# A hybrid encoder block with a mixture of experts: program order kept through the k and q projections, small copies and shifts moved between engines, and the end of the expert loop written in another order

## The chip, the cores and the metric

The kernel runs on one core of a Trainium2 chip. Times are device microseconds (us) of one execution. TensorE multiplies, VectorE, ScalarE and GpSimd do the elementwise work, and SyncE issues nearly all DMA transfers; in the profile they are PE, DVE, ACT, POOL and SP. The program of each engine is a list that the engine works off in order.

## The reference, cut to what matters

```
h = rmsnorm(x, mix_norm)                       # x: 512 rows x 1024
q, k, v, f_logit, gate_in, rec_in = split(h @ w_in)
log_f = log_sigmoid(f_logit + b_forget)
att = forgetting_attention(q, k, v, log_f)     # 8 heads of 64, causal softmax, bias by cumulated log_f
rec = causal_depthwise_conv(rec_in, conv_w, conv_b)
rec = rg_lru(rec, w_a, b_a, w_x, b_x, lam)     # gated linear recurrence over the rows
lru_out = rec * gelu(gate_in)
x = x + concat(att, lru_out) @ w_out
h2 = rmsnorm(x, ffn_norm)
# experts: 4 groups of 8; every row goes to the best group and to the best 2 experts in it
hg = silu(h2 @ w_gate[e]) * (h2 @ w_up[e])     # 1024 -> 256
y += (hg * combine[e]) @ w_down[e]             # 256 -> 1024
out = rmsnorm(x + y, final_norm)
```

All arrays are float32. The weights of the 32 experts are 100 MB, and every expert's weights are read once.

## The kernel before, in words

**Front.** The 512 rows stand as 4 tiles of 128. A product that wants full precision is made from three matmuls (`mm3`): both operands are split in a rounded high part (a copy on ScalarE, `split` by `act`) and a low part (a subtraction on VectorE or, for one tile at the start, on GpSimd), and high x high, high x low and low x high are added in PSUM. First come the rows' norm, their transposes (`hT`) and the v projection, whose weights `load_wv(half, kk)` brings in four pieces; then 16 projection chunks j of 128 columns (`chunk_gen(j)`): j = 0 to 3 feed the recurrent branch, 4 to 7 are k, 8 to 11 are q, 12 to 15 the gate. `chunk_gen(j)` loads and splits the weights of chunk j+1 (one `slot<-slot` of 128x1024 on ScalarE, one on VectorE), issues the 24 matmuls of chunk j (`ps_mm<-slot`) and then stores: `store_k` does on ScalarE, VectorE and ScalarE the three steps kS (high part), kS of the other half (low part) and kC (copy), twice; `store_q` one copy to qT. With j = 2 to 5 `gates` makes the gates of the recurrence, and from j = 8 on `next(rc)` issues a piece of the recurrence `recur()`: for each of 4 column blocks a tanh (a2th<-hold,ns), an exp (hold<-hold,s) and a square (a2th<-hold) on ScalarE and two products on VectorE, two blocks in a piece; then one square root over 128x2048 behind a load of its table; then four products and scans on VectorE.

**Attention.** There are 32 items (8 heads x 4 row tiles). For each pair of heads `stage_q` splits q: `qh` is copied by ScalarE, copied again by VectorE to the other half of the partitions (line 557, a cast), and GpSimd makes the low part `qC`. `logits` runs three matmuls, takes the row maximum on VectorE (nb), shifts it by two cumulated biases (a `TENSOR_SCALAR` of 128x1 on VectorE), and gives it to the exp on ScalarE as its bias. Then the row is normalised, transposed (ps_tr) and weighs v. Two strings of digits say how many matmul pieces of the output projection, the gate chunks and the router are put between the items.

**Experts.** The experts run as 8 "quads" of 4 experts; the last two (group 3, called light) have one set of places instead of two. A quad needs 12 MB of weights, through a ring of 18 buffers of 1 MB (slot, slot_m, slot_b): the gate and up weights (`load_gate_up`), then the down weights (`load_down`). A quad runs 8 steps k of gate and up matmuls (`gu_k`), multiplies the gated value (`hidden`, waits on ScalarE and VectorE), transposes it (`hidden_T`, ps_tr<-ident,hg), runs the down matmuls (`down`, ps<-slot,hgT), splits the result (y) and scatters it back with 0/1 matrices (`places` builds them, sT; ps_lg<-y,sT), each product added to xs by VectorE. The second half of a quad's scatter is kept back (`held`) and issued behind step k = 0 of the quad after. The last quad ends in the final norm: squares on ScalarE, a root and Newton step, and eight writes of the output (`write_out`).

**What sets the order.** Loads keep the program's order on SyncE's queue. With `pinned[0]` at 0 a scheduler sets the order of the engines' instructions; at 1 TensorE's instructions keep the program's order, at 2 those of VectorE and ScalarE that go through the helpers too. The loads of expert weights wait for ring buffers that the work before gives back.

Of the kernel before, what the change touches and what calls it, by code (L numbers as in the profile page):

```python
# [18 lines left out]
P = 128  # L19
# [34 lines left out]
def block_kernel(ctx, tc, x, mix_norm, w_in, b_forget, conv_w, conv_b, w_a, b_a, w_x, b_x, lru_lambda,  # L54
# [195 lines left out]
    raws = [load_wv(0, 0)]  # L250
    load_x(1)
    raws.append(load_wv(0, 1))
# [309 lines left out]
    def logits(qb, hd):
# [12 lines left out]
        ts(nb, nb, c1, ALU.subtract, c1, ALU.add)  # L575
# [423 lines left out]

    def places(g, q, hfs, s16):  # L1000

        n = NS * 3 if g else 12
        pt = pst("gz")
        pc = pst("tr")[:, 0:n] if len(hfs) > 1 else pt[:, 2 * P:2 * P + n]
        sq = [(2 * h + t, s16[h][:, t, q * 4:q * 4 + 4, :].rearrange("p e c -> p (e c)")) for h in hfs for t in range(2)]
        rows = [slice(e * CAP, (e + 1) * CAP) for e in range(4)]
        for i, (t, v) in enumerate(sq):
# [6 lines left out]
        sT = {}  # L1014
        for i, h in enumerate(hfs):
            sT[h] = ring_b[0].tile([P, 2, P], F32R, name=f"sT{h}", bufs=1)
            act(sT[h], pt[:, 2 * i * P:2 * (i + 1) * P].rearrange("p (t s) -> p t s", t=2), AF.Copy)
# [16 lines left out]
        return sT, cw  # L1034
# [136 lines left out]
    for i, (g, q) in enumerate(quads[:-1]):  # L1171
# [107 lines left out]
    scatter_to(pb, y0, sT[1])  # L1279
    for t in range(2):  # L1280
# [3 lines left out]
    down_mm(py1, hgT, dns[i], 1, [1])  # L1284
    y1 = split_y(py1)
    for t in range(2, 4):
        square_out(t, 0, xs[:, t, h0])
    pc, pd = ([psum("lg"), psum(tag)] for tag in ("mm", "tr"))
    scatter_to(pc, y1, sT[0])
    scatter_to(pd, y1, sT[1])  # L1290
    n0, n1 = (rsqrt_parts(hf) for hf in range(2))
    for t in range(2):
        scatter_add(pc[t], t, 1)
        square_out(t, 1, xs[:, t, h1])
    for t in range(2):
        scatter_add(pd[t], 2 + t, 1)
    i0 = next(n0)
    run(n0)
    for t in range(2, 4):
        square_out(t, 1, xs[:, t, h1])  # L1300
    write_out(0, 1, i0, xs[:, 0, h1])
    i1 = next(n1)
    run(n1)
    for t in range(NT):
        if t:
            write_out(t, 1, (i0, i1)[t // 2], xs[:, t, h1])
        write_out(t, 0, (i0, i1)[t // 2], None)
# [88 lines left out]
```

## Time and profile before

| | |
|---|---|
| median of 3 runs | 493.54 us (492.54 to 494.38) |
| profiled execution, its own time | 493.44 us |
| span of its trace | 491.6 us |
| mean granted TensorE clock | 0.983 of full speed |
| PE busy | 456.8 us, 93% of the span |
| DVE busy | 300.2 us, 61% |
| ACT busy | 200.7 us, 41% |
| POOL busy | 42.3 us, 9% |
| moved by the main DMA queue | 120.56 MB |

The shares are means over stages with different limits: the front runs to about 260 us, the experts from there to the end. The span leaves out 1.8 us of the profiled execution's time.

### The profile page before, as it was taken

The page shows a single profiled execution, that of the slowest core. Times are in us where ns is not written, and L with a number is a line of the kernel's source. Part 1 is how long each engine was busy: PE and PEld are TensorE (multiplying, and loading weights), DVE is VectorE, ACT ScalarE, POOL GpSimd, SP SyncE. Part 2 cuts the span into 40 slices and gives each one's busy share as a digit, 9 for nine tenths or more (in the row PEclk, how much of TensorE's full clock was granted, in tenths as well). Part 3 has the DMA queues.
Part 4 walks back from the last instruction along what each step waited for, and adds up shares of the span by engine and source line. Part 5 has one row for each costly group of instructions (what it writes and reads, how often), then busy time and mean ns, then how long its engine had stood idle before and what let it go on. Part 6 is the DMA issues. An engine that isn't in the chain of part 4 may idle for free.

```text
span 491.6 us, 9352 instructions
## 1 busy us (share of the span) xinstructions
PE 456.8 (93%) x3481; PEld 282.3 (57%) x3481; DVE 300.2 (61%) x768; ACT 200.7 (41%) x414; POOL 42.3 (9%) x84
## 2 busy tenths in 40 slices
PE   5999999899999999999999999999999999998880
PEld 3998777688876776668834345333354343633330
DVE  5768885653899477896675735346363363353553
ACT  6546669834685175655433123111131111211243
POOL 4500000011221012201000000000000000000040
PEclk9999999999999999999999999999999999999985
DMA  8767323042219230058879999999999999999934
GB/s 313 150 161 187 86 60 102 11 129 86 87 50 330 44 135 0 1 173 321 264 243 346 404 365 384 409 408 408 381 413 408 407 409 380 398 406 378 318 133 174
DMA packets 60883, 121.20 MB, mean 247 GB/s; under 512 B 11010, under 2 KB 29474, under 8 KB 60835
## 3 DMA queue, kind: packets, MB, share of 16 engines
q1 hardware_dynamic: 60832, 120.56, 68.9%
q8 instruction: 29, 0.48, 0.4%
q14 instruction: 20, 0.16, 0.1%
q10 hardware_dynamic: 2, 0.00, 0.0%
HBM read 118.45 MB, written 2.10 MB: 245 GB/s over the span
## 4 chain that ended last, share of the span: by engine, by line
PE 82%; DVE 10%; ACT 5%; issue 1%; DMA 1%; DVEq 0%; ACTq 0%
PE ps_mm L69 49%; PE ps_lg L69 16%; PE ps_tr L69 11%; PE ps_pv L69 3%; PE ps_tr L79 3%; ACT hold L94 1%; DVE h2l L88 1%; DVE hg L88 1%; DVE xs L82 1%; DVE nb L574 1%; DMA xs<-in_x_dram 1%; ACT kS L94 1%; DVE s L82 1%; ACT slot L94 1%; ACT hg L94 1%
## 5 line engine op out<-in xcount | busy, mean ns | idle before, releaser
L69 PE MATMUL ps_mm<-slot 128*128 128x512 f32 (+1 forms) x576 | 122.2, 371 | 3.8 <-ACT kC L94 2.3
L69 PEld LDWEIGHTS ps_mm<-slot 128*128 128x128 f32 x576 | 98.2, 196 | 23.4 <-ACT kC L94 2.7
L69 PE MATMUL ps_mm<-slot,xg 128*32 128x512 f32 x688 | 102.2, 594 | 0.0
L69 PEld LDWEIGHTS ps_mm<-slot,xg 128*32 128x32 f32 x688 | 25.7, 110 | 38.2 <-issue 36.3
L82 DVE TENSOR_TENSOR xs<-xs,ps_lg 128x512 f32<-128x512 f32 x61 | 38.1, 682 | 13.4 <-PE ps_lg L69 13.2
L82 DVE TENSOR_TENSOR slot<-slot 128x1024 fp32r<-128x1024 f32 (+1 forms) x27 | 32.7, 1221 | 12.1 <-ACT slot L94 11.9
L94 ACT ACTIVATE hg<-ps_mm 128x256 f32<-128x256 f32 x14 | 5.4, 384 | 82.4 <-PE ps_mm L69 80.3
L94 ACT ACTIVATE y<-ps_tr 128x512 fp32r<-128x512 f32 x27 | 16.1, 597 | 48.6 <-PE ps_tr L69 36.9
L69 PE MATMUL ps_lg<-y,sT 128*128 128x512 f32 x122 | 34.8, 422 | 1.1 <-ACT y L94 0.9
L69 PEld LDWEIGHTS ps_lg<-y,sT 128*128 128x128 f32 x122 | 20.6, 188 | 22.1 <-issue 10.1
L88 DVE SCALAR_TENSOR_TENSOR hg<-hg,ps_mm 128x256 f32<-128x256 f32 x14 | 5.9, 421 | 43.6 <-ACT hg L94 43.6
L558 POOL TENSOR_TENSOR qC<-qT,qh 64x128 fp32r<-64x128 f32 x32 | 21.5, 671 | 125.4 <-ACT qh L94 112.6
L82 DVE TENSOR_TENSOR y<-ps_tr,y 128x512 fp32r<-128x512 f32 x27 | 18.6, 687 | 21.0 <-ACT y L94 21.0
L69 PE MATMUL ps_lg<-s,hold 128*128 128x256 f32 x128 | 30.6, 324 | 0.6 <-ACT s L94 0.6
L94 ACT ACTIVATE slot<-slot 128x1024 fp32r<-128x1024 f32 (+1 forms) x28 | 29.1, 1055 | 2.0 <-PE ps_mm L69 1.7
L69 PE MATMUL ps_mm<-slot_m,xg 128*32 128x512 f32 x128 | 28.8, 593 | 0.0
L69 PE MATMUL ps_lg<-s,h2l 128*128 128x256 f16 x128 | 26.9, 278 | 1.5 <-DVE h2l L88 0.9
L69 PE MATMUL ps_mm<-slot,hold 128*128 128x512 f32 x96 | 26.8, 410 | 1.0 <-ACT hold L94 1.0
L69 PE MATMUL ps_tr<-slot,hgT 128*32 128x512 f32 x208 | 26.0, 606 | 0.0
L69 PE MATMUL ps_mm<-slot,oT 128*128 128x512 f32 x96 | 24.8, 404 | 1.0 <-DVE oT L82 0.9
L1093 POOL TENSOR_TENSOR slot<-xs,gfin 128x512 f32<-128x512 f32 x4 | 5.0, 1287 | 240.4 <-ACT slot L94 240.4
L94 ACT ACTIVATE pe<-ps_lg,nb 128x128 f32<-128x128 f32 (+3 forms) x32 | 16.8, 524 | 16.8 <-DVE nb L85 9.4
(244 smaller groups left out, 708.7 us busy)
## 6 DMA issues: line engine op xcount, KB each, us to landing
slot<-in_w_gate_dram SPq DMA_DIRECT2D x42, 512.0 KB, 10.1
slot<-in_w_up_dram SPq DMA_DIRECT2D x42, 512.0 KB, 10.2
slot_m<-in_w_down_dram SPq DMA_DIRECT2D x24, 512.0 KB, 10.1
slot<-in_w_down_dram SPq DMA_DIRECT2D x24, 512.0 KB, 11.3
slot<-in_w_in_dram SPq DMA_DIRECT2D x16, 512.0 KB, 4.7
slot<-in_w_out_dram SPq DMA_DIRECT2D x8, 512.0 KB, 3.8
slot<-in_w_gate_dram SPq DMA_DIRECT2D x16, 256.0 KB, 5.2
slot<-in_w_up_dram SPq DMA_DIRECT2D x16, 256.0 KB, 5.3
```

The lines of the kernel that those rows point to most:

```text
L69: pin(nc.tensor.matmul(out=out_, lhsT=lhsT, rhs=rhs, start=start, stop=stop))
L79: pin(nc.tensor.transpose(out=out_, in_=in_, identity=ident[0:n, 0:n]))
L82: return pin(nc.vector.tensor_tensor(out=out_, in0=a, in1=b, op=op), 2)
L88: pin(nc.vector.scalar_tensor_tensor(out=out_, in0=a, scalar=s, in1=b, op0=op0, op1=op1), 2)
L94: pin(nc.scalar.activation(out=out_, in_=in_, func=func, **kw), 2)
L558: nc.gpsimd.tensor_tensor(out=qC[own, 2 * hp + hh], in0=src, in1=qh[own, hh].bitcast(F32), op=ALU.subtract)
L574: nc.vector.reduce_max(out=nb, in_=pl[:, 0:n], axis=AX.X, negate=True)
L1093: nc.gpsimd.tensor_tensor(out=yo[t][:, sl], in0=src, in1=gfin[:, sl], op=ALU.mult)
```

## The change

- The two v weight pieces of the first half are loaded before row tile 1, not around it.
- From j = 4 to the end of `recur()` the program's order is kept on TensorE, VectorE and ScalarE (level 2). Before, the scheduler set it.
- In `stage_q` the second copy of q goes from VectorE to ScalarE (32 copies of 64x128). In `logits` the shift of the maximum goes from VectorE to GpSimd (32 of 128x1).
- The last quad's down weights come as whole rows of 4 KB (8 loads of 512 KB), no longer as halves of rows (16 loads of 256 KB).
- `places` is cut in two, the transposed places (`places_front`) and the combine weights (`place_weights`). In the light quads the held scatter moves from behind k = 0 to the place around `hidden_T`, and `places_front` behind it.
- In the last quad the down matmuls of both halves run j by j; the second half of row tiles 0 and 1 is added up in PSUM (`pc`: a product of the identity and xs, then the scatter), and is squared and written from there; the outputs of tiles 0 and 1 are written ahead of those of 2 and 3.

```
-    raws = [load_wv(0, 0)]
+    raws = [load_wv(0, 0), load_wv(0, 1)]
     load_x(1)
-    raws.append(load_wv(0, 1))
     hs = [norm_x(0)]
...
     for j in range(2, 12):
+        pinned[0] = 2 if j >= 4 else 0
         if j >= 8:
             next(rc, None)
         run(chunk_gen(j))
@@ -501,6 +501,7 @@
         if j < 6:
             gates(j - 2)
     run(rc)
+    pinned[0] = 0
...
             act(qh[own, hh], src, AF.Copy)
-            nc.vector.tensor_copy(out=qh[other, hh], in_=qh[own, hh].bitcast(F32))
+            act(qh[other, hh], src, AF.Copy)
             nc.gpsimd.tensor_tensor(out=qC[own, 2 * hp + hh], in0=src, in1=qh[own, hh].bitcast(F32),
                                     op=ALU.subtract)
...
         nc.vector.reduce_max(out=nb, in_=pl[:, 0:n], axis=AX.X, negate=True)
-        ts(nb, nb, c1, ALU.subtract, c1, ALU.add)
+        nc.gpsimd.tensor_scalar(out=nb, in0=nb, scalar1=c1, scalar2=c1, op0=ALU.subtract, op1=ALU.add)
...
-    def load_down(ex, halves=False):
-
+    def load_down(ex):
 
         dn = [[[], []] for _ in range(2)]
-        if halves:
-            for n in range(2):
-                for j in range(2):
-                    w = chunk().rearrange("p (e d) -> p e d", e=4)
-                    for e in range(4):
-                        load(w[:, e], wd_v[ex[e]].rearrange("o r d -> (o r) d")[j * P:(j + 1) * P, n * 512:(n + 1) * 512])
-                        dn[n][j].append(w[:, e])
-            return dn
...
+    def places_front(q, hfs, s16, pt=None):
+        pt = pst("gz") if pt is None else pt
+        for i, (t, v) in enumerate(quad_places(q, hfs, s16)):
             for r in rows:
                 mm(pt[r, i * P:(i + 1) * P], v[:, r], ident16, True, True)
+        sT = {}
+        for i, h in enumerate(hfs):
+            sT[h] = ring_b[0].tile([P, 2, P], F32R, name=f"sT{h}", bufs=1)
+            act(sT[h], pt[:, 2 * i * P:2 * (i + 1) * P].rearrange("p (t s) -> p t s", t=2), AF.Copy)
+        return sT
+
+    def place_weights(g, q, hfs, s16, pt=None):
+        n = NS * 3 if g else 12
...
         if light:
-            gu_k(0, [0])
-            held.pop()()
-            gu_k(0, range(1, 5))
-            sT, cw = places(g, q, (0, 1), sx[g, 0][0])
+            gu_k(0, range(5))
+            cw = place_weights(g, q, (0, 1), sx[g, 0][0])
             gu_k(0, range(5, KT))
-            hgT = hidden_T(hidden(pgs[0], cw))
+            hg = hidden(pgs[0], cw)
+            rest = held.pop()
+            rest([0])
+            hgT = hidden_T(hg)
+            rest([1])
+            sT = places_front(q, (0, 1), sx[g, 0][0])
             load_next()
             y0 = down(hgT, dns[i], 0)
             y1 = down(hgT, dns[i], 1)
             for hf in range(2):
                 scatter(y0, sT[hf], hf, 0)
 
-            def rest(y=y1, sT=sT):
-                for hf in range(2):
+            def rest(parts, y=y1, sT=sT):
+                for hf in parts:
                     scatter(y, sT[hf], hf, 1)
 
...
     pg = pst("gu")
     for k in range(KT):
         gate_up(pg, sx[g, 0][1], gus[i], q, [k])
-        if k == 0:
-            held.pop()()
-        if k == 2:
-            sT, cw = places(g, q, (0, 1), sx[g, 0][0])
+        if k == 4:
+            cw = place_weights(g, q, (0, 1), sx[g, 0][0])
...
     hg = hidden(pg, cw)
     act(warm, eps, AF.Sqrt)
+    rest = held.pop()
+    rest([0])
     hgT = hidden_T(hg, psum("tr"))
-    py0 = psum("mm")
-    down_mm(py0, hgT, dns[i], 0, [0])
-    down_mm(py0, hgT, dns[i], 0, [1])
-    y0 = split_y(py0)
-    py1 = psum("tr")
-    down_mm(py1, hgT, dns[i], 1, [0])
-    pa, pb = ([psum("lg"), psum(tag)] for tag in ("lg", "mm"))
-    scatter_to(pa, y0, sT[0])
+    rest([1])
+    sT = places_front(q, (0, 1), sx[g, 0][0])
+    py = [psum("mm") for _ in range(2)]
+    for n in range(2):
+        down_mm(py[n], hgT, dns[i], n, [0])
+
+    pc = [psum("lg") for _ in range(2)]
+    for t in range(2):
+        mm(pc[t], ident, xs[:, t, h1], True, False)
+    for n in range(2):
+        down_mm(py[n], hgT, dns[i], n, [1])
+    ys = [split_y(p_) for p_ in py]
+    pa, pb, pd = ([psum(a), psum(b)] for a, b in (("lg", "pv"), ("tr", "tr"), ("mm", "mm")))
+    scatter_to(pa, ys[0], sT[0])
+    scatter_to(pc, ys[1], sT[0], False)
+    scatter_to(pb, ys[0], sT[1])
+    scatter_to(pd, ys[1], sT[1])
...
+        square_out(t, 1, pc[t])
...
+        write_out(t, 1, i0, pc[t])
...
+        act(xs[:, t, h1], pc[t], AF.Copy)
```

How the instructions now stand on three engines (the names of DMA sources and PSUM buffers are the program's).

ScalarE, between the store of a k chunk and the first q chunk, before: one k chunk's stores (kS, kC) stand between the gates' tanh (hold_523, hold_524), single steps of the recurrence, the square root and the split of weights (slot).

```order
L94 ACTIVATE kC<-ps_mm 64x512
L94 ACTIVATE kS<-ps_mm 64x512
L94 ACTIVATE hold_523<-ps_lg,bh 128x512
L94 ACTIVATE hold_524<-ps_lg,bh 128x512
L94 ACTIVATE kC<-ps_mm 64x512
L94 ACTIVATE a2th<-hold_523,ns_560 128x512
L94 ACTIVATE hold_523<-hold_523,s_557 128x512
L94 ACTIVATE a2th<-hold_523 128x512
L94 ACT_TABLE_LOAD
L94 ACTIVATE hold_524<-hold_524 128x2048
L94 ACTIVATE kS<-ps_mm 64x512
L94 ACTIVATE slot<-slot 128x1024
```

ScalarE now, from the last k chunk's stores to the first copy of q (qT); two blocks of the recurrence stand ahead of the weights of chunk j = 9:

```order
L94 ACTIVATE kS<-ps_mm 64x512
L94 ACTIVATE kC<-ps_mm 64x512
L94 ACTIVATE a2th<-hold_523,ns_560 128x512
L94 ACTIVATE hold_523<-hold_523,s_557 128x512
L94 ACTIVATE a2th<-hold_523 128x512
L94 ACTIVATE a2th<-hold_523,ns_560 128x512
L94 ACTIVATE hold_523<-hold_523,s_557 128x512
L94 ACTIVATE a2th<-hold_523 128x512
L94 ACTIVATE slot<-slot 128x1024
L94 ACTIVATE qT<-ps_mm 128x512
```

The recurrence and its square root, which before lay among the k chunks, now lie among the q chunks.

SyncE at the start of the program, after against before (+ and -):

```order
 L104 DMA xs<-in_x_dram 128x1024
-L104 DMA slot<-in_w_in_dram 128x4x260
+L104 DMA slot<-in_w_in_dram 128x4x260 x2
 L104 DMA xs<-in_x_dram 128x1024
-L104 DMA slot<-in_w_in_dram 128x4x260
-L281 DMA prow<-in_conv_w_dram 16x128
```

The second v weight piece has moved ahead of row tile 1.

TensorE in the last quad, before, from its last gate and up matmuls to the first scatter:

```order
L69 MATMUL ps_mm<-slot_b,xg_4525 32x512 x2
L69 MATMUL ps_mm<-slot,xg_4525 32x512 x2
L69 MATMUL ps_tr<-ident,hg 32x128 x8
L69 MATMUL ps_mm<-slot,hgT 32x512 x8
L69 MATMUL ps_tr<-slot,hgT 32x512 x4
L69 MATMUL ps_lg<-y_5013,sT_4948 128x512
```

The same place now; y_4857 and y_4858 with sT_4786 and sT_4788 are the scatter held from the quad before:

```order
L69 MATMUL ps_mm<-slot_b,xg_4525 32x512 x2
L69 MATMUL ps_mm<-slot,xg_4525 32x512 x2
L69 MATMUL ps_lg<-y_4857,sT_4786 128x512
L69 MATMUL ps_lg<-y_4858,sT_4786 128x512
L69 MATMUL ps_lg<-y_4857,sT_4786 128x512
L69 MATMUL ps_lg<-y_4858,sT_4786 128x512
L69 MATMUL ps_tr<-ident,hg 32x128 x8
L69 MATMUL ps_lg<-y_4857,sT_4788 128x512
L69 MATMUL ps_lg<-y_4858,sT_4788 128x512
```

Four scatter matmuls now stand between the last gate and up matmul and the transposes of the gated value, and four between these and the down matmuls.

## Rows read from the trace of the kernel before

**Rows 1.** Windows: start:end, length, busy of PE, PEld, DVE, ACT, POOL, clock, DMA share, GB/s

```profile
0.00:260.00 260.00, 247.24 (x1419) 191.83 (x1423) 190.02 (x501) 150.39 (x298) 37.31 (x80) 0.99 0.46 141
260.00:460.00 200.00, 194.18 (x1934) 84.60 (x1930) 96.86 (x233) 38.45 (x87) 0.00 (x0) 1.00 1.02 394
```

**Rows 2.** Timeline of SyncE's queue near the end: the last gate and up load

```profile
450.62 0.33 SPq L104 DMA_DIRECT2D slot<-in_w_up_dram  x1
```

**Rows 3.** The load of rows 2 by itself: from issue to landing

```profile
DMA to landing us min/median/max: 10.3/10.3/10.3
```

**Rows 4.** Timeline of TensorE in the last quad (idle before and its releaser in brackets)

```profile
461.16 0.60 PE L69 MATMUL ps_mm<-slot_b,xg 128*32 128x512 f32 x2
...
464.17 0.60 PE L69 MATMUL ps_mm<-slot,xg 128*32 128x512 f32 x2
466.34 0.65 PE L69 MATMUL ps_tr<-ident,hg 128*32 128x128 f32 x16 [1.57 <-DVE hg L88]
```

**Rows 5.** Timeline of TensorE at the first v matmuls

```profile
11.59 1.23 PE L69 MATMUL ps_mm<-slot 128*128 128x260 f32 x4 [0.78 <-DVE slot L82]
```

**Rows 6.** Timeline of VectorE at the same time

```profile
9.80 1.41 DVE L88 SCALAR_TENSOR_TENSOR h<-xs,rs,ps_lg 128x512 f32<-128x512 f32 x2
11.12 0.42 DVE L82 TENSOR_TENSOR slot<-ps_tr,slot 128x256 fp32r<-128x256 f32 x1
```

**Rows 7.** Timeline of GpSimd at the same time

```profile
9.77 2.39 POOL L100 TENSOR_TENSOR slot<-slot 128x1040 fp32r<-128x1040 f32 x1 [5.56 <-ACT slot L94]
```

**Rows 8.** Timeline of TensorE from chunk j = 6 to the last q chunk

```profile
81.50 11.62 PE L69 MATMUL ps_mm<-slot 128*128 128x512 f32 x48
95.40 23.97 PE L69 MATMUL ps_mm<-slot 128*128 128x512 f32 x96 [2.28 <-ACT kC L94]
```

**Rows 9.** Windows: at the first q chunk, late in attention, in the last quad

```profile
96.00:99.00 3.00, 3.00 (x9) 2.35 (x8) 2.94 (x5) 1.14 (x2) 0.00 (x0) 0.50 0.02 5
...
210.00:220.00 10.00, 8.79 (x69) 6.46 (x69) 9.64 (x41) 5.44 (x15) 0.00 (x0) 1.00 0.70 213
468.00:471.00 3.00, 3.00 (x20) 0.75 (x16) 0.00 (x0) 0.18 (x1) 0.00 (x0) 0.51 1.04 396
```

**Rows 10.** Timeline of ScalarE in the k and q chunks

```profile
84.95 0.82 ACT L94 ACTIVATE a2th<-hold,ns 128x512 f32<-128x512 f32 x1
...
87.29 1.28 ACT L94 ACT_TABLE_LOAD   x1
88.59 1.92 ACT L94 ACTIVATE hold<-hold 128x2048 f32<-128x2048 f32 x1
...
93.69 1.04 ACT L94 ACTIVATE slot<-slot 128x1024 fp32r<-128x1024 f32 x1
...
98.42 0.59 ACT L94 ACTIVATE kC<-ps_mm 64x512 fp32r<-64x512 f32 x1 [1.86 <-DVE kS L82]
...
104.25 0.63 ACT L94 ACTIVATE qh<-qT 64x128 fp32r<-64x128 f32 x2
```

**Rows 11.** Timeline of VectorE at the same time

```profile
97.70 0.69 DVE L82 TENSOR_TENSOR kS<-ps_mm,kS 64x512 fp32r<-64x512 f32 x1
98.42 2.34 DVE L391 TENSOR_TENSOR_SCAN hold<-hold,hold 128x512 f32<-128x512 f32 x2
...
104.39 1.22 DVE L82 TENSOR_TENSOR slot<-slot 128x1024 fp32r<-128x1024 f32 x1 [1.37 <-ACT slot L94]
```

**Rows 12.** Tile nb, the shifts: ns of one, minimum/median/maximum, first and last start

```profile
L85 DVE TENSOR_SCALAR nb<-nb,cq x32: 255/270/275, 120.0 to 223.4; 128x1 f32<-128x1 f32 x32
```

**Rows 13.** Windows of line 557, VectorE's copies of q alone

```profile
200.00:220.00 20.00, 1.56 (x6) 1.00 0.35 107
```

**Rows 14.** Line 558, GpSimd's low parts of q

```profile
L558 POOL TENSOR_TENSOR qC<-qT,qh x32: 447/468/1740, 104.6 to 209.2; 64x128 fp32r<-64x128 f32 x32
```

**Rows 15.** Timeline of TensorE late in attention

```profile
215.28 0.63 PE L79 MATMUL ps_tr<-ident,pe 128*128 128x128 f32 x4 [1.21 <-DVE pe L85]
```

**Rows 16.** Timeline of ScalarE at the last split

```profile
475.26 0.60 ACT L94 ACTIVATE y<-ps_tr 128x512 fp32r<-128x512 f32 x1 [0.47 <-PE ps_tr L69]
```

More of the change, by code (lines that the diff above doesn't have):

```diff
@@ L998, in gate_up, with quad_places @@
                    gu[k][e], k == 0, k == KT - 1)
+    rows = [slice(e * CAP, (e + 1) * CAP) for e in range(4)]
     def places(g, q, hfs, s16):
-        n = NS * 3 if g else 12
         pt = pst("gz")
[L1004 to L1007, printed above, removed]
+        return places_front(q, hfs, s16, pt), place_weights(g, q, hfs, s16, pt)
+    def quad_places(q, hfs, s16):
+        return [(2 * h + t, s16[h][:, t, q * 4:q * 4 + 4, :].rearrange("p e c -> p (e c)")) for h in hfs for t in range(2)]
+    def places_front(q, hfs, s16, pt=None):
+        pt = pst("gz") if pt is None else pt
+        for i, (t, v) in enumerate(quad_places(q, hfs, s16)):
             for r in rows:
                 mm(pt[r, i * P:(i + 1) * P], v[:, r], ident16, True, True)
+        sT = {}
[5 more added lines that the diff above has]
+        n = NS * 3 if g else 12
+        pc = pst("tr")[:, 0:n] if pt is None else pt[:, 2 * P:2 * P + n]
+        sq = quad_places(q, hfs, s16)
         for i, (t, v) in enumerate(sq):
@@ L1013, in places @@
                 mm(pc[r], v[:, r], c, i == 0, i == len(sq) - 1)
[L1014 to L1017, printed above, removed]
         cw = moe[0].tile([P, 1], F32, name=f"cw{hfs[0]}")
@@ L1033, in places @@
             nc.vector.reduce_sum(out=cw, in_=cj, axis=AX.XY)
-        return sT, cw
+        return cw
     def hidden(pg, cw):
@@ L1180, in load_next @@
             gus[i + 1] = load_gate_up(ex, 4)
-            dns[i + 1] = load_down(ex, i + 2 == len(quads))
+            dns[i + 1] = load_down(ex)
         if light:
-            gu_k(0, [0])
-            held.pop()()
-            gu_k(0, range(1, 5))
-            sT, cw = places(g, q, (0, 1), sx[g, 0][0])
+            gu_k(0, range(5))
+            cw = place_weights(g, q, (0, 1), sx[g, 0][0])
             gu_k(0, range(5, KT))
-            hgT = hidden_T(hidden(pgs[0], cw))
+            hg = hidden(pgs[0], cw)
[4 more added lines that the diff above has]
+            sT = places_front(q, (0, 1), sx[g, 0][0])
             load_next()
@@ L1207, in block_kernel @@
                 if k == 0:
-                    held.pop()()
+                    held.pop()(range(2))
             if i == 1:
@@ L1242, in block_kernel, with rest @@
         y11 = down(hgT1, dns[i], 1)
-        def rest(y10=y10, y11=y11, sT=sT1[1]):
-            scatter(y10, sT, 1, 0)
-            scatter(y11, sT, 1, 1)
+        def rest(parts, y10=y10, y11=y11, sT=sT1[1]):
+            for n in parts:
+                scatter((y10, y11)[n], sT, 1, n)
         held.append(rest)
@@ L1255, in block_kernel @@
         gate_up(pg, sx[g, 0][1], gus[i], q, [k])
-        if k == 0:
-            held.pop()()
-        if k == 2:
-            sT, cw = places(g, q, (0, 1), sx[g, 0][0])
+        if k == 4:
+            cw = place_weights(g, q, (0, 1), sx[g, 0][0])
     gfin = ring_b[0].tile([P, D], F32, name="gfin", tag="xg1", bufs=1)
@@ L1267, in block_kernel @@
     act(warm, eps, AF.Sqrt)
+    rest = held.pop()
+    rest([0])
     hgT = hidden_T(hg, psum("tr"))
-    py0 = psum("mm")
-    down_mm(py0, hgT, dns[i], 0, [0])
-    down_mm(py0, hgT, dns[i], 0, [1])
-    y0 = split_y(py0)
-    py1 = psum("tr")
-    down_mm(py1, hgT, dns[i], 1, [0])
-    pa, pb = ([psum("lg"), psum(tag)] for tag in ("lg", "mm"))
-    scatter_to(pa, y0, sT[0])
+    rest([1])
[14 more added lines that the diff above has]
+    scatter_to(pd, ys[1], sT[1])
+    n0, n1 = (rsqrt_parts(hf) for hf in range(2))
     for t in range(2):
         scatter_add(pa[t], t, 0)
-    scatter_to(pb, y0, sT[1])
-    for t in range(2):
         square_out(t, 0, xs[:, t, h0])
@@ L1283, in block_kernel @@
         scatter_add(pb[t], 2 + t, 0)
[L1284 to L1291, printed above, removed]
+        square_out(t, 1, pc[t])
+    scatter_add(pd[0], 2, 1)
+    i0 = next(n0)
     for t in range(2):
-        scatter_add(pc[t], t, 1)
-        square_out(t, 1, xs[:, t, h1])
+        square_out(2 + t, 0, xs[:, 2 + t, h0])
+    run(n0)
     for t in range(2):
[L1296 to L1301, printed above, removed]
+        write_out(t, 1, i0, pc[t])
+        if t == 0:
+            scatter_add(pd[1], 3, 1)
+    for t in range(2):
+        square_out(2 + t, 1, xs[:, 2 + t, h1])
     i1 = next(n1)
+    for t in range(2):
+        write_out(t, 0, i0, None)
     run(n1)
[L1304 to L1307, printed above, removed]
+    for t in range(2):
+        write_out(2 + t, 1, i1, xs[:, 2 + t, h1])
+        write_out(2 + t, 0, i1, None)
+    for t in range(2):
+        act(xs[:, t, h1], pc[t], AF.Copy)
     pinned[0] = 0
```

## The prediction

> **What bounds the kernel now.** I read the windows first. Up to 260 us PE is busy for 247 us and the DMA engines for under half of the time; from 260 to 460 us the DMA share is 1.02 at 394 GB/s while PE is busy for 194 of 200 [rows 1]. So the front is PE's, with about 13 us of stalls to be had, and the experts have two bounds that lie close together. Which ends last is seen at the end of the queue: the last gate and up load is issued at 450.62 and lands 10.3 later, at 460.9 [rows 2, 3], and PE uses that weight buffer (slot_b) first at 461.16 [rows 4]. PE and DMA are level there. A gain in the front still counts in full, because the expert loads wait for buffers that PE's progress gives back, so the whole stream moves with the front; a gain of PE alone within the experts only ends in a wait for that load.
>
> The sum is made on the profiled execution's 493.44 us, 0.1 under the median of 493.54. About 0.5%, 2.5 us, is what a measurement of this kernel tells from no change.
>
> **Start (v weights before row tile 1): −1.6.** PE's long v run begins at 11.59, after a wait for VectorE's low part of hT [rows 5]. That low part starts at 11.12, behind the norm of row tile 1, two products that take from 9.80 to 11.12 [rows 6]. Meanwhile GpSimd splits the second weight piece from 9.77 to 12.16, after 5.56 idle [rows 7]. With the pieces exchanged, tile 1 lands later, its norm falls behind the low part (gain up to 1.3 to 1.5), and the split begins earlier by about the same; but tile 1 is then the late one. I take −1.6; bounds −0.5 (the next wait follows at once) and −2.0.
>
> **Program order through k and q: +3.4.** Before, the recurrence's ScalarE steps lay among the k chunks, where PE did not wait. The 96 q matmuls begin at 95.40 after 2.28 idle and end at 119.37 [rows 8]; the clock stood at 0.50, the 1.2 GHz level, from 96 to 99, after that idle time [rows 9], so some 1.7 of the 23.97 is clock, and one matmul at full clock is (23.97 − 1.7)/96 = 0.232. The 48 matmuls before them end at 81.50 + 48 × 0.232 = 92.6. From there to 119.4 are 26.8 us.
>
> Now the same stretch in program order, from T = 0 at the last k matmul. ScalarE: kS 0.59, VectorE's part 0.69 and a gap, kC 0.59, and all this twice (the second kS beside VectorE's first part) makes 3.8 [rows 10, 11]. Then two blocks of the recurrence: from the tanh at 84.95 to the table load at 87.29 one block took 2.34 [rows 10], so 4.7, and the split of chunk 9's weights, 1.04: 9.6. VectorE's low part, 1.22 [rows 11], makes 10.9. PE meanwhile has only chunk 8, 24 × 0.232 = 5.6, so it idles for 4 to 5 us where it idled for 2.28. Chunk 9 then takes 5.6 and, as before behind such a gap, 1.6 for the clock. ScalarE goes on with qT 0.6, two more blocks 4.7 and four copies of q (0.31 each, [rows 10]): 16.1, weights of chunk 10 at 17.2, low part 18.4, which PE awaits hardly. Then qT, the table 1.28, the root 1.92 and the split 1.04 bring chunk 11's weights to 22.5 and the low part to 23.7; PE runs that chunk to 29.1. Behind it VectorE has four products and scans (0.63 and 1.15 each, [rows 11]) ahead of the low part of chunk 12: PE passes there at about 31.3, having done by then some 1.4 of work that before came after 119.4 (first logits, transposes, two matmuls). So 29.9 + 0.2 for odds against 26.8: I take +3.4. Bounds: +2 if the scheduler's order had hidden costs that go (the 1.86 wait of kC is one, [rows 10]), +5 if the clock falls a second time.
>
> **Attention (casts to ScalarE, shifts to GpSimd): −4.0.** VectorE loses 32 shifts of 0.270 [rows 12], 8.6, and 32 casts of 1.56/6 = 0.26 [rows 13], 8.3. ScalarE gains 32 × 0.31 = 10 [rows 10], but from 210 to 220 it is busy for 5.4 of 10 where VectorE is for 9.6 [rows 9]; there PE's transposes wait for VectorE's normalised row, 1.21 at 215.28 for one [rows 15]. In the stretch from 201 to 216 six casts (1.56) and some seven shifts (1.9) lie on that path, of which I take 3.0; one more microsecond for the waits of the earlier items. Against it: the shift now passes from VectorE to GpSimd to ScalarE, one more crossing. GpSimd's price for a 128x1 shift has no row; its nearest one on these tiles is qC, 64x128, 0.447 at least and 1.740 at most [rows 14], and VectorE's 0.27 is the other end. I take 0.3 to 0.4, since the tile is one column and not 128, which adds a latency that the matmul pieces between the items cover, except where the chain is already late. Bounds: −8 (all of 16.9 beside the path's half), 0 (each step's latency eats its gain).
>
> GpSimd's qC took 0.447 at the least and 1.740 at the most for one shape [rows 14], so it is held at times. The Trainium skill, page "SBUF — State Buffer", section "SBUF: two separate sides", says that VectorE and GpSimd share a port pair as an exclusive lock, and that the loser waits for a whole instruction. It speaks against this move; the trace agrees that GpSimd is held at times. By it the shift would at worst cost 1.3 more (1.740 − 0.447) in each of the items whose chain is late, ten such items being 13.
>
> **Front together.** −1.6 + 3.4 − 4.0 = −2.2, which moves PE and the load stream alike.
>
> **Last quads and tail: −0.9.** In the last quad the eight held scatter matmuls go from behind k = 0 into the wait of 1.57 before the transposes at 466.34 [rows 4]; the light quad before has the same wait and the same filling. PE so comes to k = 4 some 3 to 4 us before its weights, which the queue brings no earlier than the front's shift: that gain is a wait. From the landing at 460.9, nine steps of 0.43 (461.16 to 464.17, [rows 4], with the last) end at 464.4 at full clock, at 465.7 if the clock is halved after the wait. The gated value takes its 1.57 again: transposes at 466.0 to 467.3, 466.34 before. Behind them PE was at 0.51 of the clock from 468 to 471, 3.0 busy of 3.0 [rows 9]; now scatters fill the wait ahead of it, so that stretch should run at 1.00, −1.5 for the same work. Down matmuls now come first for both halves, with two identity products of 512 float32 columns between them, 0.4 (as two steps of 0.232) to 1.7 (as eight steps of 0.21); I take 1.7. The last split, at 475.26 before [rows 16], comes at 472.7 to 473.9; after it there is more to do, all of eight scatters and two more additions of about 0.7 (as the subtraction in [rows 11]): +1.6. The sum lies between −1.0 and +0.2; the first outputs leave earlier, so I take −0.9; bounds −2.1 and +1. The down weights in whole rows cost nothing and give nothing: they are asked for after the gate and up load that PE waits for.
>
> **Sum.** 493.44 − 2.2 − 0.9 = 490.3 us.
>
> **Rivals.** *ScalarE binds* (slower): from the last k store to the end of attention each item's exp stands behind the added copies in ScalarE's fixed order, and behind GpSimd's shift. If attention gives nothing back (0) and k and q cost +5.0: −1.6 + 5.0 − 0.9 = +2.5, 495.9. It decides once shift and copies make an item's chain longer by the 0.5 that VectorE saves on it (0.27 + 0.26); ScalarE's 5.4 of 10 speaks against it, the 1.740 of qC for it. *No change*: attention gives only 1.5 and the wait for k = 4 halves the clock in the gate and up steps, so that the tail gives +0.3: −1.6 + 3.4 − 1.5 + 0.3 = +0.6, and with a middle value of k and q somewhat less: about 493. For it speaks that the loads are level with PE. *Much faster*: no second stall in q, +2, attention at −6.5, start −1.6, tail −1.3: −7.4, 486.0. For it speaks VectorE's 9.6 of 10; against it, that half of its work there is not on the path.
>
> **Chances.** Forecast 0.42, with a range of its own from 487.5 to 492; no change 0.24; much faster 0.20; slower 0.14. Faster by over 0.5% (under 491.0) come the much faster case and most of the forecast's, with little of the no-change case: 0.56; within 0.5%: 0.30; slower: 0.14. The range, 485.5 to 495.5, leaves out the ends of the fastest and the slowest case.
>
> **What the trace would show.** Start: the long v run begins near 10, without a wait for hT's low part. k and q: an idle of 4 to 5 us on PE at chunk 9, half clock behind it, a second short wait at chunk 12; if PE has no gap there, this step is wrong. Attention: VectorE under 9 of 10 late in attention, transposes that don't wait for normalised rows, and shifts on GpSimd below 0.5; shifts over 1 us and exps waiting for GpSimd mean the slower rival. End: PE waits for DMA at k = 4 of the last quad, scatters stand where the 1.57 was, and the clock is 1.00 in the down matmuls; if the last gate and up load lands earlier by other than the front's shift, the coupling of stream and front is wrong.

## The result and the profile after

The changed kernel takes 508.46 us (507.91 to 510.16, 4 runs) against 493.04 of the kernel before beside it: ratio 1.0314, 95% interval 1.0281 to 1.0348. It is slower by 3%, outside the range and on the other side, and 12.6 above the slowest rival of the prediction (495.9).

One row divides the loss by stages: the expert matmuls of the gate and up steps (ps_mm<-slot,xg, called the row on xg below). Its first start ends the front, and its last matmul ends the experts. Before:

```profile
L69 PE MATMUL ps_mm<-slot,xg x688: 592/592/617, 245.5 to 464.2; 128*32 128x512 f32 x172
```

After:

```profile
L69 PE MATMUL ps_mm<-slot,xg x688: 589/592/617, 255.8 to 480.8; 128*32 128x512 f32 x172
```

The front ends 10.3 later, the experts take 225.0 and not 218.7, 6.3 more, and from there to the end of the span it is 27.7 (508.5 − 480.8) against 27.4. Of the 16.9 by which the two spans differ, 10.3 lie in the front, 6.3 in the experts and 0.3 in the tail. The windows after, in the columns of [rows 1] and [rows 9]:

```profile
100.00:109.00 9.00, 8.21 (x29) 6.33 (x30) 5.04 (x6) 7.59 (x14) 1.04 (x2) 0.81 0.21 58
...
121.00:140.00 19.00, 16.77 (x71) 12.70 (x70) 14.29 (x23) 10.34 (x24) 4.87 (x6) 0.91 0.57 194
...
164.00:171.00 7.00, 7.00 (x24) 5.37 (x24) 4.09 (x12) 4.52 (x16) 2.25 (x5) 0.58 0.42 147
0.00:255.80 255.80, 239.45 (x1302) 188.66 (x1302) 166.77 (x398) 153.42 (x319) 55.63 (x112) 0.97 0.42 129
255.80:481.00 225.20, 212.25 (x2096) 92.06 (x2095) 106.83 (x273) 44.23 (x98) 0.00 (x0) 1.00 0.99 372
484.00:490.00 6.00, 6.00 (x55) 1.88 (x53) 1.52 (x3) 0.88 (x3) 0.00 (x0) 1.00 0.40 158
```

TensorE is idle for 13 us in the experts (225.2 − 212.25; 5.8 in 200 us before, [rows 1]), and the clock is below 1 in three stretches of the front, each behind a gap. The down stretch of the last quad, at 0.51 before [rows 9], is at 1.00. What ended TensorE's gaps, by total, times and longest:

```profile
PE ps_lg L69 <- ACT sT L94: 8.7, 12, 1.0
PE ps_mm L69 <- ACT slot L94: 3.5, 1, 3.5
PE ps_lg L69 <- ACT pe L94: 2.6, 1, 2.6
PE ps_mm L69 <- DVE slot L82: 2.4, 4, 1.3
...
PE ps_pv L69 <- DVE hg L88: 1.0, 1, 1.0
```

The greatest, 12 waits for the copy sT, did not exist before and stands in no part of the prediction. Some of it takes the place of other waits: those for the gated value (hg) were 4.1 before and are 1.0 now. One wait for sT in TensorE's timeline, and the copies themselves, which take 0.38:

```profile
272.02 0.30 PE L69 MATMUL ps_lg<-ident,s 128*32 128x128 f16 x8
273.29 0.22 PE L69 MATMUL ps_lg<-c,s 128*32 128x12 f16 x8 [0.97 <-ACT sT L94]
```

```profile
L94 ACT ACTIVATE sT<-ps_lg x16: 378/378/388, 272.9 to 485.4; 128x256 fp32r<-128x256 f32 x16
```

The places (ident,s) are written to PSUM, and the combine weights (c,s) wait until ScalarE has copied the places out. In `places` before, both groups of matmuls came first and the copies behind them; `places_front` now ends with the copies, and `place_weights` writes another part of the same buffer behind them, in each of the 12 calls for two-set quads. The front's gaps, on TensorE:

```profile
9.13 4.81 PE L69 MATMUL ps_mm<-slot 128*128 128x260 f32 x24
...
100.27 0.73 PE L69 MATMUL ps_mm<-slot 128*128 128x512 f32 x2 [3.47 <-ACT slot L94]
101.52 7.38 PE L69 MATMUL ps_mm<-slot 128*128 128x512 f32 x24 [0.53 <-DVE slot L82]
...
121.73 0.73 PE L69 MATMUL ps_mm<-slot 128*128 128x512 f32 x2 [0.62 <-ACT qT L94]
122.80 0.97 PE L69 MATMUL ps_mm<-slot 128*128 128x512 f32 x3 [0.33 <-DVE slot L82]
125.05 8.54 PE L69 MATMUL ps_mm<-slot 128*128 128x512 f32 x29 [1.28 <-DVE slot L82]
...
163.29 0.58 PE L69 MATMUL ps_lg<-kS,qh 128*128 128x256 f32 x1 [2.58 <-ACT pe L94]
```

The wait at the start [rows 5] is gone, and the first 24 v matmuls take 4.81 where 22 took 5.13 before:

```profile
11.59 5.13 PE L69 MATMUL ps_mm<-slot 128*128 128x260 f32 x22 [0.78 <-DVE slot L82]
```

The second q chunk waits 4.0 (3.47 and 0.53) for its weights, and the 24 matmuls behind these waits take 7.38 instead of 5.6; the first gate chunk waits 2.2 in three pieces; at 163 the logits wait for a PSUM buffer whose exp is late. ScalarE in the q chunks:

```profile
90.74 0.59 ACT L94 ACTIVATE kS<-ps_mm 64x512 fp32r<-64x512 f32 x1 [0.60 <-PE ps_mm L69]
...
94.10 0.59 ACT L94 ACTIVATE kC<-ps_mm 64x512 fp32r<-64x512 f32 x1 [0.76 <-DVE kS L82]
94.72 0.81 ACT L94 ACTIVATE a2th<-hold,ns 128x512 f32<-128x512 f32 x1
...
99.17 1.04 ACT L94 ACTIVATE slot<-slot 128x1024 fp32r<-128x1024 f32 x1
...
109.09 1.28 ACT L94 ACT_TABLE_LOAD   x1
...
114.45 1.28 ACT L94 ACT_TABLE_LOAD   x1
115.75 0.37 ACT L94 ACTIVATE pe<-ps_lg,nb 128x128 f32<-128x128 f32 x1
```

The split of chunk 9's weights comes at 99.17, behind stores and two blocks of the recurrence, as predicted; not in the prediction is the second table load, back for the exp, at 114.45. The gate chunk's last two waits, to 122.80 and 125.05, each end with a low part on VectorE:

```profile
121.53 1.21 DVE L82 TENSOR_TENSOR slot<-slot 128x1024 fp32r<-128x1024 f32 x1
122.67 1.21 DVE L390 TENSOR_TENSOR_SCAN hold<-hold,hold 128x512 f32<-128x512 f32 x1
123.80 1.19 DVE L82 TENSOR_TENSOR slot<-slot 128x1024 fp32r<-128x1024 f32 x1
```

A scan of the recurrence stands between the two low parts, and VectorE has no idle time from 113.28 to there. The shifts on GpSimd, with what waited for them, and one of the longest beside VectorE's work (answers to [rows 12]):

```profile
L576 POOL TENSOR_SCALAR nb<-nb,cq x32: 357/368/1847, 109.7 to 234.6; 128x1 f32<-128x1 f32 x32
...
  ACT pe L94: 23.8, 19
```

```profile
148.99 1.85 POOL L576 TENSOR_SCALAR nb<-nb,cq 128x1 f32<-128x1 f32 x1 [1.77 <-DVE nb L575]
```

```profile
148.85 1.23 DVE L82 TENSOR_TENSOR slot<-slot 128x1024 fp32r<-128x1024 f32 x1
150.00 0.69 DVE L88 SCALAR_TENSOR_TENSOR gxg<-gxg 128x512 f32<-128x512 f32 x1
```

A shift takes 0.37 in the median, but 1.85 where VectorE is at work on two instructions of two inputs, a subtraction and a product, from 148.85 to 150.69; the shift ends at 150.84. Four of the 32 take over 1 us, all between 125 and 158. ScalarE's exps waited 23.8 us for these shifts, and 9.4 for VectorE's shifts before. The Trainium skill, page "SBUF — State Buffer", section "SBUF: two separate sides", says that the loser of the port pair waits for the whole instruction; these rows agree. The shift ahead of the gap at 163 is not one of the four:

```profile
161.39 0.41 DVE L575 TENSOR_REDUCE nb<-ps_lg 128x1 f32<-128x256 f32 x1
```

```profile
161.98 0.66 POOL L576 TENSOR_SCALAR nb<-nb,cq 128x1 f32<-128x1 f32 x1 [0.20 <-DVE nb L575]
```

```profile
162.67 0.47 ACT L94 ACTIVATE pe<-ps_lg,nb 128x256 f32<-128x256 f32 x1 [1.63 <-POOL nb L576]
```

TensorE is idle from 160.71 to 163.29. VectorE's maximum comes 0.7 behind the last matmul, then the shift takes 0.66, and the exp ends at 163.14.

The end, answers to [rows 4] and [rows 16]:

```profile
477.63 0.59 PE L69 MATMUL ps_mm<-slot,xg 128*32 128x512 f32 x1 [1.29 <-DMA slot<-in_w_up_dram]
...
482.90 0.65 PE L69 MATMUL ps_tr<-ident,hg 128*32 128x128 f32 x16 [0.42 <-DVE hg L88]
...
486.66 1.98 PE L69 MATMUL ps_lg<-xs,ident 128*128 128x512 f32 x4
```

```profile
490.56 0.60 ACT L94 ACTIVATE y<-ps_mm 128x512 fp32r<-128x512 f32 x1 [0.18 <-PE ps_mm L69]
```

The wait of 1.57 before the transposes is 0.42, the wait for the last load is there (1.29), the identity products take 1.98; the last split comes 9.8 behind the last gate and up matmul (490.56 − 480.8), 11.1 before (475.26 − 464.2).

### The profile page after: what moved, and what is told of

It is laid out like the page before. It is cut to its first block, busy times and chain, and to the rows that moved or that the text cites. A ratio compares the mean times of both kernels' runs of the same rounds, so it can differ in the third digit from the quotient of the medians.

```text
span 508.5 us, 9371 instructions
## 1 busy us (share of the span) xinstructions
PE 464.9 (91%) x3485; PEld 287.1 (56%) x3485; DVE 287.4 (57%) x702; ACT 210.4 (41%) x448; POOL 60.6 (12%) x116
## 4 chain that ended last, share of the span: by engine, by line
PE 73%; ACT 10%; DVE 6%; DMA 5%; issue 2%; POOL 2%; SPq 0%; ACTq 0%; DVEq 0%; POOLq 0%
PE ps_mm L69 41%; PE ps_lg L69 16%; PE ps_tr L69 10%; DMA slot<-in_w_up_dram 4%; PE ps_pv L69 3%; PE ps_tr L79 3%; ACT slot L94 2%; POOL nb L576 1%; DVE hold L390 1%; ACT qh L94 1%; ACT hold L94 1%; DVE slot L82 1%; ACT hg L94 1%; DVE hold L82 1%; ACT sT L94 1%
## 5 line engine op out<-in xcount | busy, mean ns | idle before, releaser
L69 PE MATMUL ps_mm<-slot 128*128 128x512 f32 (+1 forms) x576 | 123.9, 373 | 6.7 <-ACT slot L94 3.5
L82 DVE TENSOR_TENSOR xs<-xs,ps_lg 128x512 f32<-128x512 f32 x57 | 35.7, 682 | 12.2 <-PE ps_lg L69 12.2
L69 PE MATMUL ps_mm<-slot,hold 128*128 128x512 f32 x96 | 28.8, 433 | 0.9 <-DVE hold L82 0.5
L94 ACT ACTIVATE pe<-ps_lg,nb 128x128 f32<-128x128 f32 (+3 forms) x32 | 16.8, 525 | 24.1 <-POOL nb L576 23.8
L576 POOL TENSOR_SCALAR nb<-nb,cq 128x1 f32<-128x1 f32 x32 | 18.6, 581 | 59.0 <-DVE nb L575 39.7
```

What stands on the lines that cost most here:

```text
L69: pin(nc.tensor.matmul(out=out_, lhsT=lhsT, rhs=rhs, start=start, stop=stop))
L82: return pin(nc.vector.tensor_tensor(out=out_, in0=a, in1=b, op=op), 2)
L94: pin(nc.scalar.activation(out=out_, in_=in_, func=func, **kw), 2)
L576: nc.gpsimd.tensor_scalar(out=nb, in0=nb, scalar1=c1, scalar2=c1, op0=ALU.subtract, op1=ALU.add)
```

## The experiments

Every ratio is to the kernel before, timed beside it, with its 95% interval. That kernel itself spread from 489.7 to 495.7 us over 29 runs, so that small single gains are read from ratios of many runs. Against the changed kernel (508.46, 1.0314) up to three differences are given: of the medians, of the ratios (× 493), and of the fronts, which the row on xg shows in one profile each. The kernel of e8 has the front of the kernel before, and its row starts at 242.6 where that one's starts at 245.5, so that a difference of two fronts may be off by some 3 us.

**e1, e10: the places.** e1:

```
-        return places_front(q, hfs, s16, pt), place_weights(g, q, hfs, s16, pt)
+        ...
```

In place of the last line stands the body of `places` as before: both groups of matmuls, then the copies sT.

> The changed kernel, with the places of the two-set quads in the old order again: both groups of matmuls first, the copies sT behind them. Waits theory: TensorE idled 8.7 us in front of the combine-weight matmuls, each time until ScalarE had copied sT out of the same PSUM buffer; these waits go, and the time falls by 5 to 8.5, to 500 to 503.5. Stream theory: from 280 us on the DMA share is 1.02, the weight stream sets the end and the waits lie beside it; the time falls by less than 1.5, to 507 or more.

502.45 us, 1.0247 (1.0214 to 1.0280): 6.0 less than the changed kernel, 3.3 by the ratios. The experts take 218.4, as before the change, and there is no wait for sT.

```profile
L69 PE MATMUL ps_mm<-slot,xg x688: 591/592/617, 254.7 to 473.1; 128*32 128x512 f32 x172
```

e10:

```
-        pt = pst("gz")
-        return places_front(q, hfs, s16, pt), place_weights(g, q, hfs, s16, pt)
+        return places_front(q, hfs, s16), place_weights(g, q, hfs, s16)
```

> The changed kernel with the combine weights' product of the two-set quads in a PSUM buffer of its own; the order stays as changed (places, copies sT, weights). Buffer theory: TensorE waited only because the product went into the buffer that ScalarE was still copying sT from; the 8.7 of idle before ps_lg<-c,s go, the time falls by 4 to 7 as in e1. Order theory: it waits for the copies themselves, or for the buffer that takes its place: less than 1.5.

502.93 us, 1.0187 (1.0141 to 1.0232), experts 219.9 (255.6 to 475.5). That is 5.5 less than the changed kernel, 6.3 by the ratios. In the same order, with another buffer, the 8.7 are gone. So it is the shared buffer, not the copy's turn. The stream theory falls: the experts get shorter by 6.6 (e1) although the DMA share was 0.99, and the loads run at 387 GB/s there, at 372 in the changed kernel. Of the 8.7, 2.4 come back as waits for the gated value (3.4 in e1, 1.0 in the changed kernel), so that some 6.3 were to be had.

**e2, e11, e13: the fixed order.** e2:

```
-        pinned[0] = 2 if j >= 4 else 0
```

> The changed kernel without the program order for j from 4 on (level 0 as before). Waits theory: TensorE's idle of 4.3 at the second and third q chunk, 2.2 more at the first gate chunk and half clock for 1.8 us of work go, against 2.3 idle that comes back at the first q chunk; the time falls by 3.5 to 6, to 502.5 to 505. Attention theory: the front's loss is that of the shifts on GpSimd, whatever the order; the time changes by less than 1.5.

500.92 us, 1.0205 (1.0175 to 1.0236): 7.5 less than the changed kernel, 5.4 by the ratios, the front 7.8 shorter.

```profile
L69 PE MATMUL ps_mm<-slot,xg x688: 591/592/617, 248.0 to 471.6; 128*32 128x512 f32 x172
```

e11:

```
-        if j >= 8:
+        if j >= 6:
             next(rc, None)
```

> The changed kernel, still in program order from j = 4, with the recurrence's pieces issued from j = 6 instead of 8, so that tanh, exp, square and root stand among the k chunks as the scheduler had them. Place theory: not the fixed order costs but what stands in it, eight us of recurrence and two table loads ahead of the q chunks' weights; TensorE's gaps of 3.5 to 4.3 at the second q chunk go and the time falls by 4 to 8. Order theory: any fixed order blocks ScalarE behind its waits for VectorE in the k stores; less than 2.

512.17 us, 1.0377 (1.0327 to 1.0427): 3.7 more than the changed kernel. The place theory, as I put it, fell: a gap of 3.4 now stands at a k chunk, where the stores are longer than in q, and two of 1.9 and 2.7 follow.

```profile
87.42 8.70 PE L69 MATMUL ps_mm<-slot 128*128 128x512 f32 x24 [3.40 <-ACT slot L94]
97.48 0.74 PE L69 MATMUL ps_mm<-slot 128*128 128x512 f32 x2 [1.35 <-ACT slot L94]
```

These waits were again for the split behind stores and recurrence, so e13 moved that split alone:

```
+        chunk_j = chunk_gen(j)
         if j >= 8:
             next(rc, None)
-        run(chunk_gen(j))
+        run(chunk_j)
```

> The changed kernel, still in program order from j = 4, with the split of the next chunk's weights issued ahead of the piece of the recurrence and no longer behind it. Split theory: the gaps come from this split standing behind stores and recurrence, 3.8 + 4.7 + 1.0 + 1.2 against the 5.6 of one chunk's matmuls; ahead of the recurrence it is done at 6, TensorE's gaps at the q chunks fall from 4.3 to 1 or 2 with the half clock behind them, the time falls by 3 to 6. Order theory: a fixed order costs because each engine waits in it for the other, wherever the split stands: less than 1.5.

500.74 us, 1.0183 (1.0146 to 1.0220): 7.7 less than the changed kernel, 6.5 by the ratios, as much as without any fixed order and more than I expected.

```profile
91.33 11.44 PE L69 MATMUL ps_mm<-slot 128*128 128x512 f32 x48 [0.27 <-DVE slot L82]
102.99 5.41 PE L69 MATMUL ps_mm<-slot 128*128 128x512 f32 x22 [0.21 <-DVE slot L82]
108.62 0.73 PE L69 MATMUL ps_mm<-slot 128*128 128x512 f32 x2 [0.23 <-ACT slot L94]
```

The gaps at the q chunks shrink to 0.2 to 0.3, and from 91 to 120 the clock is 1.00. A fixed order is not dear as such; the place of one split in it is.

**e3, e4, e7, e9: attention.** e3 puts the shift back on VectorE, e4 the second copy of q:

```
-        nc.gpsimd.tensor_scalar(out=nb, in0=nb, scalar1=c1, scalar2=c1, op0=ALU.subtract, op1=ALU.add)
+        ts(nb, nb, c1, ALU.subtract, c1, ALU.add)
```

```
-            act(qh[other, hh], src, AF.Copy)
+            nc.vector.tensor_copy(out=qh[other, hh], in_=qh[own, hh].bitcast(F32))
```

> The changed kernel with the shift of the maximum on VectorE again. Waits theory: exp on ScalarE waited 23.8 us for GpSimd's shift and TensorE 2.6 for an exp at 163, with half the clock behind it; undone, TensorE gains 3 to 6, the time falls to 502.5 to 505.5. Order theory: the front's loss is the order through k and q alone, and the shift on VectorE only fills VectorE again; less than 1 either way.

501.28 us, 1.0221 (1.0188 to 1.0255): 7.2 less than the changed kernel, 4.6 by the ratios. The front is 8.0 shorter. Up to 140 us the exps of both profiles start within 0.4 of each other; from 160 to 172 TensorE is busy for 12.0 of 12.0 us (9.4 in the changed kernel), so the gap at 163 is gone, and the exps wait 7.4 us for the shift.

```profile
L69 PE MATMUL ps_mm<-slot,xg x688: 590/592/617, 247.8 to 471.9; 128*32 128x512 f32 x172
```

> The changed kernel with the second copy of q on VectorE again. Waits theory: ScalarE is busy for 12 to 15 of 20 us there and nothing on TensorE waited for these copies but 0.6 at a copy of qT; between 1 faster and 1 slower. If ScalarE binds in attention: 2 to 4 faster.

511.9 us, 1.0437 (1.0404 to 1.0469): slower by 3.4, 6.1 by the ratios, where I expected 1 at most; the front is longer by only 0.8. So the copies on ScalarE are a gain, of a size that these figures leave open. e7 makes that change alone, in the kernel before:

```
-            nc.vector.tensor_copy(out=qh[other, hh], in_=qh[own, hh].bitcast(F32))
+            act(qh[other, hh], src, AF.Copy)
```

> The kernel before with the second copy of q on ScalarE and nothing else. In the changed kernel this copy was worth 5 to 6. Theory that VectorE's chain holds TensorE in attention: 2 to 5 faster, the waits for VectorE's row at 207 and 215 shrink. Rival: the 5 to 6 are only there while the shift goes over GpSimd, which the casts on VectorE held up; then under 1 here.

490.43 us, 0.9951 (0.9926 to 0.9975): a gain without the shift on GpSimd too, of some 2.4 (1.2 to 3.6). The exps wait 2.9 us for VectorE's shift, 9.4 before.

**e5, e8: start and end alone**, in the kernel before. e5:

```
-    raws = [load_wv(0, 0)]
+    raws = [load_wv(0, 0), load_wv(0, 1)]
     load_x(1)
-    raws.append(load_wv(0, 1))
```

> The kernel before with the two v weight pieces ahead of row tile 1 and nothing else. Waits theory: the long v run starts about 1.1 to 1.6 earlier, as in the changed kernel (24 matmuls from 9.13 on without a wait), and the whole time falls by 0.8 to 1.6. Rival: row tile 1 is late by as much and the gain is given back within the v projection: under 0.4.

489.65 us, 0.9940 (0.9919 to 0.9961): a gain of 3.0 (1.9 to 4.0), more than I expected.

e8 is written as the changed kernel with all but `load_down`, the light quads and the tail taken back, `places` as in e1:

```
-    raws = [load_wv(0, 0), load_wv(0, 1)]
+    raws = [load_wv(0, 0)]
     load_x(1)
+    raws.append(load_wv(0, 1))
...
-        pinned[0] = 2 if j >= 4 else 0
...
-            act(qh[other, hh], src, AF.Copy)
+            nc.vector.tensor_copy(out=qh[other, hh], in_=qh[own, hh].bitcast(F32))
...
-        nc.gpsimd.tensor_scalar(out=nb, in0=nb, scalar1=c1, scalar2=c1, op0=ALU.subtract, op1=ALU.add)
+        ts(nb, nb, c1, ALU.subtract, c1, ALU.add)
```

> The kernel before with the end of the change alone: whole rows of down weights, held scatter beside the gated values, the last quad's tail; places of the two-set quads in the old order. Stream theory: TensorE comes early to the last quad's weights and waits there (some 1 to 2 idle for the last gate and up load), the last split is no earlier: between 1 faster and 1 slower. If the waits of 1.6 in the light quads count in full: 2 to 4 faster.

493.28 us, 1.0026 (0.9999 to 1.0053): between no change and 2.6 slower, so no gain. TensorE waits 1.60 for the last up load, as forecast:

```profile
457.32 0.59 PE L69 MATMUL ps_mm<-slot,xg 128*32 128x512 f32 x1 [1.60 <-DMA slot<-in_w_up_dram]
```

**e6, e9, e12, e14: together.** e6 is the changed kernel with the edits of e1, e2 and e3, e12 the kernel before with those of e5 and e7, as their diffs above show them.

> The changed kernel with the three repairs together: places in the old order, no program order through k and q, shift on VectorE. Additive theory: the three single gains (4 + 5 + 4.5 by the runs so far) add to 13, and the rest of the change (start, copies on ScalarE, last quads) is about even: ratio to the kernel before 1.00 to 1.01. Overlap theory: the waits stand in for each other, what one frees the next takes: 1.012 or more. If copies on ScalarE and the end are gains of their own: under 0.995.

486.16 us, 0.9888 (0.9853 to 0.9922). The front ends at 239.0; 255.8 less 7.8 (e2) less 8.0 (e3) would be 240.0: the gains add. Against the changed kernel it gains 22.3, 21.0 by the ratios; the single steps give 22.4 by the rows (6.6, 7.8, 8.0), 20.7 by the medians and only 13.3 by the ratios, so that the ratios of e1 to e3 seem to make the steps too small. ScalarE's exps wait for the shift 2.9 us, 23.8 in the changed kernel:

```profile
  ACT pe L94: 2.9, 4
```

> The kernel before with the two single gains, the start and the second copies of q on ScalarE, and nothing of the end. If gains add: 0.994 and 0.995 give 0.989, as e6, so the end gives nothing; if the end gives a gain in e6 that e8 hid: 0.990 to 0.993.

487.2 us, 0.9878 (0.9843 to 0.9912). e9 and e14 are e6 and e12 with this left out:

```
-        ts(nb, nb, c1, ALU.subtract, c1, ALU.add)
```

> The repaired kernel (e6) with the shift of the maximum left out altogether: it subtracts and adds the same bias, so only a rounding of the exponent's offset is left out, which the softmax divides out again. Chain theory: what made the shift on GpSimd dear is that it stands in the chain from the maximum to the exp; then leaving it out also gains, 0.3 to 0.6 per item whose chain is late: 1 to 3 faster than e6. Rival: in e6 VectorE's chain is no longer what TensorE waits for; within 1 of e6.

485.74 us, 0.9848 (0.9814 to 0.9882).

> The kernel before with the start, the second copies of q on ScalarE, and without the shift of the maximum (a rounding of the exponent's offset left out, as in e9); its end as before. If the gains add and the changed end gives nothing: 0.983 to 0.987, as e9. If the changed end gives a gain: 0.988 to 0.990.

484.49 us, 0.9884 (0.9841 to 0.9926). The four can't be told apart by their ratios. e14's lies where I expected it if the changed end gave a gain, but its interval holds both cases, and e6, with the changed end, is by its ratio no faster than e12 without it. The fronts end at 239.0 (e6) and 236.7 (e9), 239.9 (e12) and 237.4 (e14): leaving the shift out shortens them by 2.3 and 2.5, in one profile each and so within the 3 us of doubt. By their medians e9 is within 0.5 of e6, so that its two theories stay undecided. All four beat both kernels, and 0.9940 × 0.9951 = 0.9891 is what start and copies give; the changed end adds nothing that shows.

## Why the prediction was wrong, by its steps

Three steps failed: the price of the shift, the size of the order's cost, and the places, which I had put at nothing.

- **Not in the sum: the places.** I read the cut of `places` for the light quads, where it moves work, and not for the other 12 calls, where it puts ScalarE's copy between two products of one PSUM buffer. +6.6 by e1 (225.0 − 218.4), and e10 shows the buffer as the cause. The Trainium skill, page "PSUM — Partial Sum Buffer", section "PSUM bank collisions raise a hardware error", says to guard PSUM by bank and quadrant and not by address: such a write behind a copy has to wait even where the regions are apart. By it the wait was to be expected; e1 and e10 agree.
- **What bounds the kernel: half right.** "A gain of PE alone within the experts only ends in a wait for that load" held (e8). A loss of PE there does count, because the loads wait for its buffers; I used that coupling for the front's shift alone.
- **Attention, −4.0: the step that failed most is the price of the shift.** I took 0.3 to 0.4, which is the median, for all 32, and covered the rest with matmul pieces. The exps came late for two reasons that the rows show: shifts of up to 1.85 beside VectorE's work, and a chain from the maximum to the exp that got longer even with a shift of 0.66 (163). With the exp, the logits' PSUM buffer is late, and TensorE pays there with 2.6 of waiting and a half clock (0.58 from 164 to 171, 2.9 of 7.0): 5.5 of the 8.0 by which e3's front is shorter; where the rest arises is open. So the shift cost +4.6 to +8.0 (e3: 4.6 by the ratios, 7.2 by the medians, 8.0 by the fronts), where some −2.2 of the −4.0 was meant for it, by the shares of 1.9 and 1.56. The casts, some −1.8, measured −2.4 (e7). VectorE's relief came as forecast (busy for 14.0 of the 20 us from 200 to 220, 18.8 before). The slower rival had the mechanism in its text ("behind GpSimd's shift") and a chance of 0.14, and the sign that I named for it came: shifts over 1 us, and exps that wait for GpSimd. Its attention term, 0, was still too small by 2 to 6.
- **k and q, +3.4: right in mechanism and first gap, wrong in size.** The gap of 4 to 5 at the second q chunk is there (4.0), with half the clock behind it, and the idle time at the first gate chunk is 2.2 as in my timeline (31.3 − 29.1). But the last of its three waits ends at 125.05, 34.3 behind the end of the last k matmul (90.7), where I had 31.3: a low part stood behind one more scan. (By my own terms the first low part comes at 23.7 + 4 × 1.78 + 1.22 = 32.0, and it did, at 122.74.) And the clock fell once more (0.91 from 121 to 140), the condition that I gave for the bound of +5. Measured are 5.4 to 7.8 (e2), above that bound. What the table load back for the exp (1.28) cost, no run shows. e13 shows that the split's place behind the recurrence makes all of it.
- **Start, −1.6:** right in sign and mechanism, too small: 3.0 by e5 (1.9 to 4.0), where my bound was 2.0. The first v matmuls ran faster, too, at a clock of 1.00 in both kernels; why, no run shows.
- **End, −0.9:** the wait moved from the transposes to the load, as forecast, and the down stretch runs at 1.00. The last split is earlier by 1.3, just under the 1.4 to 2.6 of the sum, and the chain behind it longer by 1.6, as in the sum; I took a value near the better end for the outputs that leave earlier, and that gain did not come: the tail takes 27.7 where it took 27.4, and e8 is no faster.

By the rows, start −3.0, casts −2.4, order +7.8, shifts +8.0, places +6.6 and end 0 add to +17.0; the spans differ by 16.9, the medians by 15.4. Two small slips of my sum have no weight in this: 29.9 + 0.2 − 26.8 is 3.3 and not 3.4, and nine steps of 0.43 from 460.9 end at 464.8 and not 464.4.

## What to carry to other kernels

When a helper is cut in two, read every caller: a copy out of PSUM between two products of one buffer is waited for each time, here 0.73 in the mean (8.7 / 12) for a copy of 0.38. In a fixed order, look per chunk at what stands ahead of the next chunk's operands, and put their preparation first; whether order or scheduler sets it matters less. A tiny instruction in the chain to a late consumer has to be priced by its longest time beside a busy neighbour and by what stands ahead of it, not by its median.

## What the runs showed of the hardware

A 128x1 instruction on GpSimd took 0.36 at the least and 1.85 at the most for the same shape, against 0.26 to 0.28 on VectorE [rows 12]; the four over 1 us lie over VectorE's two-input instructions. Gaps on TensorE of 3.5 and 0.5, of 2.2 in three pieces, and of 2.6 were followed by the 1.2 GHz level (0.50 from 102 to 105, from 126 to 128 and from 163.3 to 169; the stretches above hold the means 0.81, 0.91 and 0.58). Gaps of 0.2 to 0.3 (e13) and the twelve of up to 1.0 in the experts, where the clock is 1.00, were not. No run here tells what part of the shift's cost the port, what part the extra crossing between engines, and what part GpSimd's own low parts of q ahead of a shift make.
